# Order of four pieces of work around the mixer's end and the routing stage of an encoder layer

## The chip, the cores and the metric

The kernel runs on one core of a Trainium2 chip. The metric is the device time of one execution in microseconds (us), the median of three runs. The engines are named as in the profile: PE (matrix multiply, with PEld for its weight loads), DVE (vector), ACT (scalar, activation), POOL (GpSimd) and SP, which here only issues DMAs and reads a few registers for them.

## The reference, cut to what matters

```
mod = silu(c) @ w_ada + b_ada                   # six rows of 2048: sh1, sc1, g1, sh2, sc2, g2
h   = rms_norm(x, g_mix) * (1 + sc1) + sh1
z   = h @ w_in                                  # 2048 x 4616; the last 8 columns are the forget logits fz
y   = concat[gmlp(u, v), pool(p), forgetting_attention(q, k, va, fz)]      # the mixer
x   = x + g1 * (y @ w_out)
h   = rms_norm(x, g_ffn) * (1 + sc2) + sh2
scores = sigmoid(h @ w_router); top group of 4, then top 2 of its 4 experts, per token
x   = x + g2 * moe(h)                           # 16 experts: (silu(h @ e_gate) * (h @ e_up)) @ e_down
```

There are 256 tokens of 2048 values, 16 experts with an inner width of 1024, everything in float32. The output is x.

## The kernel before

**Stages.** In time order: (1) the first modulation rows, then the product with w_in, in five chunks of rows of w_in (256, 256, 512, 512, 512 rows, `CHUNKS`); (2) the mixer, woven into the last chunk (`LAST` is its order); (3) the product with w_out, four column blocks of 512, each from four loads of 512 rows (`wout_steps(n)`, steps `g`); (4) the router: norm, logits, choice, counts of tokens per expert, and a gather of the tokens into the order of the experts; (5) the experts, fifteen of them one after the other (`ORDER`), each with eight 2 MB loads of e_gate and e_up and four of e_down.

**Precision.** Products with w_in and w_out are made as three matmuls in a rounded format. ACT casts a weight tile to its high part, and DVE or POOL subtracts that from the tile for the low part (`split`, lines 175 and 176, tile `whl`, 128x2x512, six buffers). `WSO = "GVGG"` says which engine subtracts for the four rows of w_out's tile: POOL, DVE, POOL, POOL. One such step is six matmuls of 128x512 on PE (`mm3`, twice).

**Weights in flight.** Loads go through a ring of half buffers of 1 MB (`ring()`, `load_tile`, line 147), `ring0` to `ring2` with two halves each, and from stage 3 on also `ringm0`. A load into a half waits until what was in it has been read. In stage 5 the same buffers are used whole (2 MB), with two more (`ringl0`, `ringl1`) that take the place of the gather's inputs and so can be filled only when the gather is done. SP issues all weight loads, in program order.

**What sets the order.** Each engine runs its own list of instructions in program order, and the list follows the order of the Python code. A small queue, `todo`, holds matmul parts back: `step(prep, run)` runs `prep` at once (the load and the splits) and puts `run` (the matmuls) at the end of `todo`; while what is in it weighs over `LOOK = 4` (a split step 1, an unsplit one 2, anything else 0), the first entry is taken out and run. `then(f)` puts other work behind what waits there. `flush()` runs all.

**Forget logits.** `make_h(q)` (line 408) makes one chunk of h: per 128 columns, PE transposes, DVE scales (`hf`, line 420), ACT casts and DVE subtracts (`hT`). The 8 forget logits are small matmuls from `hf` into `lgp` (`late`), put into `todo` behind two entries.

**Gate 2.** The row g2 takes 16 loads of w_ada (sixteen unsplit steps, four per 512 columns; each is four matmuls with one output row, and every fourth step a bias matmul behind it and an ACT copy `r2[q]`). `G2 = [1, 2, 1, 1]` steps go beside the last block of w_out, `G2_MID = 1` behind it, `NG2` of them are put in ahead of the count matmuls, and `g2_run(16)` puts in the rest ahead of the gather. Because `todo` holds two unsplit steps back, the last two of those ahead of the counts run behind them. The broadcast of g2 to 128 rows (`g2w`: four matmuls with `sel` and four ACT copies) is first needed in the first expert's down stage.

**Counts.** The matmuls with `M` (the chosen experts) into `pp`, then `po`, give the order of the experts (`irow`, line 1089), which SP reads into a register before it can issue the first expert's load.

Of the kernel before, what the change touches and what calls it, by code (L numbers as in the profile page):

```python
# [63 lines left out]

LAST = ["mwm", "mwm", "mw", "mawmam", "amw", "mmmwammm", "ammam", "ammammgmx", "amvammm", "aamsmapmtmmmm"]

G2, G2_MID, NG2 = [1, 2, 1, 1], 1, 4

M1A, M1B, M2A, M2B, G1 = "PPVV", "PPPP", "PPPP", "PPPP", "PVVV"
WSPLIT, WSO = ["VGVG", "VGVG", "GVGG", "GVGG", "GVGG"], "GVGG"  # L70
# [12 lines left out]
def layout(tiles):  # L83
    out, o = {}, 0
    for key, r0, nr, c0, ncol in tiles:
        m = nr * ncol // 128
        out[key] = (o, m, r0, nr, c0, ncol)
        o += 128 * m
    return out
# [19 lines left out]
WOUT = layout(((n, g), 512 * g, 512, 512 * n, 512) for n in range(4) for g in range(4))  # L109
# [7 lines left out]
def body(tc, x_d, prm_d, bg_d, wada_d, win_d, wout_d, egu_d, ed_d, out_d):  # L117
# [32 lines left out]
    todo = deque()  # L150

    def run_first():
        f, x, _ = todo.popleft()
        f(x) if x is not None else f()
# [6 lines left out]
    def then(f):  # L161
        todo.append((f, None, False)) if todo else f()

    def flush():
        while todo:
            run_first()

    V, S, G, E = nc.vector, nc.scalar, nc.gpsimd, nc.tensor

    def mm(out, lhsT, rhs, start=True, stop=True):  # L170
        E.matmul(out, lhsT=lhsT, rhs=rhs, start=start, stop=stop, skip_group_check=True)  # L171
# [35 lines left out]
    sel = cst.tile([128, 128], F32, name="sel")  # L207
# [26 lines left out]
    pbanks = deque(psM.tile([128, 512], F32, name=f"pm{i}") for i in range(3))  # L234

    def pm():
        pbanks.rotate(-1)
        return pbanks[-1]
# [122 lines left out]
    def yhi(k):  # L361
        return hTs[0][:, (k - 8) // 4, k % 4, :] if k >= 8 else hTs[1][:, k // 4, k % 4, :]
# [22 lines left out]
    for g, w in enumerate((2, 4, 8, 16)):  # L385
        b = band0[:, g, :]
# [20 lines left out]
    def make_h(q):  # L407
        k0, nk = CHUNKS[q]
        hq = hbuf(q)
        ts = []  # L410
        for c in range(nk):
            k = k0 + c
            if c % 2 == 0:
                p2 = pt()
                for j in range(4):
                    o = 128 * (c + j // 2)
                    E.transpose(p2[:, 128 * j:128 * j + 128], xn[:, j % 2, o:o + 128], ident)
            p = p2[:, 256 * (c % 2):256 * (c % 2) + 256]
            t = wk.tile([128, T], F32, name="hf", bufs=5)
            V.tensor_scalar(t, p[:, :T], mod[:, 1, k:k + 1], mod[:, 0, k:k + 1], op0=OP.mult, op1=OP.add)  # L420
            split(hq[:, 0, c, :], hq[:, 1, c, :], t)
            ts.append((k, t))

        def late():
            for k, t in ts:
                o = 32 * (k % 4)
                mm(fzp[o:o + 8, :], wfz[:, k, :], t, start=k < 4, stop=k >= KD - 4)
        todo.insert(2, (late, None, False)) if todo else late()


    def halves(flat, tile, engs, xs, banks, first, last, after):
        buf = []

        def one(a):
            def prep():
                if a == 0:
                    w = ring()
                    load_tile(w, flat, tile)
                    buf.append(w.rearrange("p (k n) -> p k n", k=4))
                hl = hp.tile([128, 2, 512], F32R, name="whl")  # L440
                split(hl[:, 0], hl[:, 1], buf[0][:, a, :], engs[a])
                return hl

            def run(hl):
                P = banks()
                for h in range(2):
                    mm3(P[h], *xs(a, h), hl[:, 0], hl[:, 1], first and a == 0, last and a == 3)
                if a == 3:
                    after(P)
            step(prep, run, True)  # L450
        for a in range(4):
            one(a)
# [300 lines left out]
    ylo = py.tile([128, KD, T], F32R, name="ylo")  # L753
# [11 lines left out]
    def att(n):  # L765
        for _ in range(min(n, len(steps_a))):
            then(lambda i=steps_a.popleft(): att_step(i))

    for i, order in enumerate(LAST):
        if i < len(PIECES):  # L770
            piece(last, PIECES[i])
        for c in order:
            if c == "a":
                att(1)
            elif c == "m":
                mods(1)
            elif c == "w":
                for f in work.get(PIECES[i], ()):
                    then(f)
            else:  # L780
                then(named[c])
    att(11)
    mods(len(mod2))
    flush()
    while tbanks[-1] is not accs[0]:
        tbanks.rotate(-1)
    tbanks.pop()
# [60 lines left out]
    for w in (128, 64, 32, 0):  # L848
        n = CAPS.count(w)
# [2 lines left out]
    limR = rtile([128, 16], "limR")  # L852
    V.tensor_scalar(limR, capR, -1.0, 512.0, op0=OP.mult, op1=OP.add)

    WO = [{"V": V, "G": G}[c] for c in WSO]

    def wout_steps(n, Ps):
        def banks():
            if not Ps:
                Ps.extend(sets[n % 2])  # L860
            return Ps

        def one(g):
            def xs(c, h):
                k, s = 4 * g + c, slice(128 * h, 128 * h + 128)
                return yhi(k)[:, s], ylo[:, k, s]
            return lambda: halves(wout_d, WOUT[n, g], WO, xs, banks,
                                  g == 0, g == 3, lambda P: None)
        return [one(g) for g in range(4)]

    def x1_block(n, Ps, g1):
        for h in range(2):
            t = wk2.tile([128, 512], F32, name="xg")
# [63 lines left out]

    g1_load(1)
    pbanks.append(accs[1])
    sets = [list(pbanks)[:2], list(pbanks)[2:]]  # L940
    r2, g2p, g1s = [], deque(), {}

    def g2_run(n):
# [1 line left out]
            step(*g2p.popleft())  # L945

    for n in range(4):
        Ps = []
        ws = wout_steps(n, Ps)
        for g in range(4):  # L950
            ws[g]()
            if n + g:
                g1_load(1)
            if n == 3 and g == 0:
                r2 += [grow2() for _ in range(4)]
                for q in range(4):
                    g2p.extend(ada_parts(5, 4 * q, 4, lambda P, q=q: S.copy(r2[q], P), (accs[0], sets[0][0])[q % 2],
                                         4 + q))
            if n == 3:
                for _ in range(G2[g]):  # L960
                    step(*g2p.popleft())
            if n == 0 and g == 3:
                then(logit_const)
            if n == 3 and g == 2:
                then(lambda: S.activation(lnj, ones[:, 0:1], AF.Ln))
            if g == 1 and n > 0:
                then(lambda n=n: logit_a(n - 1))
            if g == 2:
                then(lambda n=n: g1s.__setitem__(n, g1_bc(n)))
                if n > 0:  # L970
                    then(lambda n=n: logit_b(n - 1))
        then(lambda n=n, Ps=Ps: x1_block(n, Ps, g1s[n]))
# [14 lines left out]
    g2w = pg2.tile([128, D], F32, name="g2w")  # L987
# [130 lines left out]

    g2_run(16)
    flush()  # L1120

    for b in range(4):
        p = pm()
        mm(p, sel, r2[b])
        S.copy(g2w[:, 512 * b:512 * b + 512], p)
    def gather(k):

        p = pm()
# [54 lines left out]
    for h in range(2):  # L1183
# [4 lines left out]
        pick(gatO[:, h, :], ohO, gatR[:, h, :])  # L1188
        V.tensor_tensor(posR[:, h, :], posR[:, h, :], dlt, op=OP.add)

    s_phl.close()
    pl, s_pl = pool("pl", 1, side="right")
    wides += [pl.tile([128, 2 * RINGW], F32, name=f"ringl{i}") for i in range(RING_LAST)]
# [269 lines left out]
```

## Time and profile before

| | |
|---|---|
| median of three runs | 1419.65 us (1417.56 to 1420.41) |
| profiled execution | 1422.95 us, span 1421.1 us |
| PE busy | 1209.0 us, 85% of the span |
| DVE, ACT, POOL busy | 590.9, 363.6, 216.1 us |
| DMA | 539.14 MB, mean 379 GB/s |
| TensorE clock, mean granted | 0.957 |

The profile is one execution. Times are us from the span's start. In a timeline a row gives start, length, engine, source line, operation, what is written from what, how many instructions are merged, and in brackets how long the engine had been idle before and what released it. A granted clock of 1.00 is 2.4 GHz and 0.50 is 1.2 GHz. Line 171 is the helper of all matmuls, lines 175 and 176 those of all splits, so tile names tell what a row is.

### The profile page before, as it was taken

The numbers are of one execution on the slowest core, as the hardware profiler recorded it, in microseconds if no ns is written. First come the engines' busy times: TensorE is split into PE (matmuls) and PEld (weight loads), VectorE is DVE, ScalarE is ACT, GpSimd is POOL, SyncE is SP. The second block draws the span as 40 slices with busy tenths as digits, with TensorE's granted clock in tenths as the row PEclk, the third lists the DMA queues.
The fourth block names the chain that finished last, engine by engine and source line by source line (L and its number), as shares of the span: only waits on it lengthen the run. The fifth ranks groups of instructions, "written<-read, shape, count | busy, mean of one in ns | idle before, by whom it ended". The sixth has DMA issues, their size and how long they took to land.

```text
span 1421.1 us, 17044 instructions
## 1 busy us (share of the span) xinstructions
PE 1209.0 (85%) x6646; PEld 628.8 (44%) x6646; DVE 590.9 (42%) x1121; ACT 363.6 (26%) x661; POOL 216.1 (15%) x170
## 2 busy tenths in 40 slices
PE   5999999999899787999969999688885888858866
PEld 2656766665676352763326743222232222322221
DVE  4366544655784734882327942121130211302112
ACT  4633433445444241770006820000000000000000
POOL 1345654522675000000000000000000000000000
PEclk9999999999999898999989999899998999989997
DMA  9988695889979689998999989999999999999996
GB/s 390 362 342 336 255 369 217 309 341 354 366 306 368 218 370 428 427 380 355 427 426 427 423 310 429 425 427 427 427 426 427 427 427 428 426 427 427 426 427 266
DMA packets 49222, 539.14 MB, mean 379 GB/s; under 512 B 5472, under 2 KB 5600, under 8 KB 7024
## 3 DMA queue, kind: packets, MB, share of 16 engines
q1 hardware_dynamic: 47664, 534.79, 92.0%
q10 hardware_dynamic: 1472, 3.19, 0.6%
q8 instruction: 55, 0.90, 0.3%
q14 instruction: 31, 0.25, 0.1%
HBM read 535.86 MB, written 2.10 MB: 379 GB/s over the span
## 4 chain that ended last, share of the span: by engine, by line
PE 56%; DMA 33%; DVE 4%; issue 3%; ACT 2%; POOL 1%; SPq 0%; DVEq 0%; POOLq 0%; ACTq 0%
PE lbank L171 25%; PE pm L171 18%; DMA ring<-in_e_down_dram 13%; DMA ringm<-in_e_gu_dram 10%; DMA ring<-in_e_gu_dram 9%; PE ada L171 6%; PE bank L171 4%; PE pt L171 1%; DMA ring<-in_w_ada_dram 1%; POOL whl L176 1%; DVE el L176 0%; DVE hf L420 0%; PE pt L327 0%; DMA bgt<-in_bg_dram 0%; ACT hT L175 0%
## 5 line engine op out<-in xcount | busy, mean ns | idle before, releaser
L171 PE MATMUL pm<-whl,hT 128*128 128x512 f32 x1056 | 278.6, 401 | 10.0 <-DVE whl L176 6.9
L171 PEld LDWEIGHTS pm<-whl,hT 128*128 128x128 f32 x1056 | 198.1, 191 | 74.2 <-issue 11.0
L171 PE MATMUL lbank<-ring,xr 128*32 128x256 f32 (+1 forms) x1216 | 158.3, 505 | 44.0 <-DMA ring<-in_e_gu_dram 44.0
L176 POOL TENSOR_TENSOR whl<-ring,whl 128x512 fp32r<-128x512 f32 x116 | 159.3, 1393 | 178.1 <-ACT whl L175 173.8
L171 PE MATMUL bank<-y,gt 128*128 128x512 f32 x240 | 119.6, 621 | 0.0
L171 PEld LDWEIGHTS lbank<-ring,xr 128*32 128x32 f32 (+1 forms) x1216 | 56.3, 130 | 137.8 <-issue 66.2
L1344 DVE TENSOR_TENSOR xa<-xa,bank 128x512 f32<-128x512 f32 x120 | 82.5, 688 | 74.4 <-PE bank L171 74.4
L171 PE MATMUL lbank<-ringl,xr 128*32 128x256 f32 (+1 forms) x608 | 81.4, 520 | 35.5 <-DMA ringl<-in_e_gu_dram 35.5
L175 ACT CAST whl<-ring 128x512 fp32r<-128x512 f32 x164 | 94.6, 621 | 60.8 <-PE pm L171 47.3
L171 PE MATMUL lbank<-ring,hidT 128*64 128x512 f32 (+1 forms) x416 | 84.9, 716 | 28.4 <-DVE hidT L1303 16.7
L1335 DVE TENSOR_TENSOR y<-lbank,g2w 128x512 f32<-128x512 f32 x60 | 41.5, 692 | 154.4 <-PE lbank L171 154.4
L171 PE MATMUL lbank<-el,xs 128*128 128x512 f32 x384 | 94.3, 405 | 7.1 <-ACT el L175 5.2
L171 PE MATMUL lbank<-ringm,xr 128*32 128x256 f32 (+1 forms) x608 | 75.7, 472 | 21.7 <-DMA ringm<-in_e_gu_dram 20.8
L1231 ACT COPY gt<-bank 128x256 f32<-128x256 f32 x15 | 5.6, 372 | 337.7 <-PE bank L1229 337.7
L1285 DVE TENSOR_TENSOR hid<-hid,lbank 128x512 f32<-128x512 f32 x11 | 7.6, 688 | 201.8 <-PE lbank L171 201.7
L171 PEld LDWEIGHTS lbank<-el,xs 128*128 128x128 f32 x384 | 73.6, 194 | 27.8 <-ACT el L175 7.4
L460 DVE TENSOR_TENSOR z<-z,pm 128x512 f32<-128x512 f32 x72 | 49.1, 688 | 68.9 <-PE pm L171 68.9
L171 PE MATMUL ada<-ring,cact 128*1 128x512 f32 (+1 forms) x520 | 62.5, 580 | 17.4 <-DMA ring<-in_w_ada_dram 14.2
L171 PE MATMUL lbank<-ringl,hidT 128*64 128x512 f32 (+1 forms) x416 | 74.2, 598 | 1.3 <-DMA ringl<-in_e_down_dram 1.3
L171 PEld LDWEIGHTS bank<-y,gt 128*128 128x128 f32 x240 | 41.9, 192 | 74.1 <-issue 71.7
L1280 DVE TENSOR_TENSOR hid<-hid,lbank 128x256 f32<-128x256 f32 x6 | 2.5, 422 | 165.5 <-PE lbank L171 140.0
L171 PEld LDWEIGHTS lbank<-ringl,xr 128*32 128x32 f32 (+1 forms) x608 | 28.8, 133 | 86.9 <-DMA ringl<-in_e_gu_dram 50.7
(389 smaller groups left out, 1264.1 us busy)
## 6 DMA issues: line engine op xcount, KB each, us to landing
ring<-in_e_gu_dram SPq DMA_DIRECT2D x60, 2048.0 KB, 24.6
ring<-in_w_ada_dram SPq DMA_DIRECT2D x81, 1024.0 KB, 7.3
ringm<-in_e_gu_dram SPq DMA_DIRECT2D x30, 2048.0 KB, 25.5
ringl<-in_e_gu_dram SPq DMA_DIRECT2D x30, 2048.0 KB, 25.0
ring<-in_e_down_dram SPq DMA_DIRECT2D x30, 2048.0 KB, 24.7
ringl<-in_e_down_dram SPq DMA_DIRECT2D x30, 2048.0 KB, 25.8
ring<-in_w_in_dram SPq DMA_DIRECT2D x28, 1024.0 KB, 7.1
ring<-in_w_out_dram SPq DMA_DIRECT2D x12, 1024.0 KB, 8.2
```

What stands on the lines that cost most here:

```text
L171: E.matmul(out, lhsT=lhsT, rhs=rhs, start=start, stop=stop, skip_group_check=True)
L175: S.copy(hi, src)
L176: (eng or V).tensor_tensor(lo, src, hi.bitcast(F32), op=OP.subtract)
L460: V.tensor_tensor(dst, dst, P[h], op=OP.add)
L1231: S.copy(gt, p[:, :256])
L1280: V.tensor_tensor(hid[:, :256], hid[:, :256], P[1][:, :256], op=OP.mult)
L1285: V.tensor_tensor(hid[:, o], hid[:, o], P[2 * b + 1], op=OP.mult)
L1335: V.tensor_tensor(y, P, g2w[:, c0:c0 + 512], op=OP.mult)
L1344: V.tensor_tensor(a, a, p, op=OP.add)
```

## The change

Four edits. (1) `late` goes into `todo` behind six entries instead of two. (2) `wout_steps` and its list are made earlier, and the first of block 0's four steps is called ahead of the mixer's end: its load and its four splits are put in there, and its matmuls stay in `todo` until the mixer's matmuls are through (the loop takes the place of `flush()`). Its two PSUM banks are drawn there (`pair0`) and kept as one of the two sets. (3) `NG2` is 8 instead of 4. (4) The broadcast of g2 stands behind the gather and the rest of the routing arithmetic instead of ahead of them.

```diff
-G2, G2_MID, NG2 = [1, 2, 1, 1], 1, 4
+G2, G2_MID, NG2 = [1, 2, 1, 1], 1, 8
...
-        todo.insert(2, (late, None, False)) if todo else late()
+        todo.insert(6, (late, None, False)) if todo else late()
...
+    def wout_steps(n, Ps):
+        def banks():
+            if not Ps:
+                Ps.extend(pair0 if n == 0 else sets[n % 2])
+            return Ps
...
     att(11)
     mods(len(mod2))
-    flush()
+
+    Ps0, pair0 = [], [pm(), pm()]
+    ws0 = wout_steps(0, Ps0)
+    ws0[0]()
+    while len(todo) > 4 or todo[0][1] is None:
+        run_first()
...
-    sets = [list(pbanks)[:2], list(pbanks)[2:]]
+    sets = [pair0, [t for t in pbanks if not any(t is x for x in pair0)]]
...
     for n in range(4):
-        Ps = []
-        ws = wout_steps(n, Ps)
+        Ps = [] if n else Ps0
+        ws = wout_steps(n, Ps) if n else ws0
         for g in range(4):
-            ws[g]()
+            if n + g:
+                ws[g]()
...
     g2_run(16)
     flush()
-
-    for b in range(4):
-        p = pm()
-        mm(p, sel, r2[b])
-        S.copy(g2w[:, 512 * b:512 * b + 512], p)
     def gather(k):
...
+    for b in range(4):
+        p = pm()
+        mm(p, sel, r2[b])
+        S.copy(g2w[:, 512 * b:512 * b + 512], p)
     s_phl.close()
```

What this does to the engines' lists is shown at three places. First PE, where the third chunk of h is made: the last two split steps of the old chunk, the forget logits (`lgp`), and the first steps of the new one (`hT1`). Before:

```order
L171 MATMUL pm1_120<-whl_723,hT0_132 128x512 x3
L171 MATMUL pm2_121<-whl_723,hT0_132 128x512 x3
L171 MATMUL lgp_117<-hf_762,prm1_69 8x256
L171 MATMUL lgp_117<-hf_766,prm1_69 8x256
L171 MATMUL lgp_117<-hf_774,prm1_69 8x256
L171 MATMUL lgp_117<-hf_778,prm1_69 8x256
L171 MATMUL pm0_119<-whl_735,hT1_133 128x512 x3
L171 MATMUL pm1_120<-whl_735,hT1_133 128x512 x3
L171 MATMUL pm0_119<-whl_744,hT1_133 128x512 x3
L171 MATMUL pm1_120<-whl_744,hT1_133 128x512 x3
```

and now:

```order
L171 MATMUL pm1_120<-whl_723,hT0_132 128x512 x3
L171 MATMUL pm2_121<-whl_723,hT0_132 128x512 x3
L171 MATMUL pm0_119<-whl_735,hT1_133 128x512 x3
L171 MATMUL pm1_120<-whl_735,hT1_133 128x512 x3
L171 MATMUL pm0_119<-whl_744,hT1_133 128x512 x3
L171 MATMUL pm1_120<-whl_744,hT1_133 128x512 x3
L171 MATMUL pm0_119<-whl_747,hT1_133 128x512 x3
L171 MATMUL pm1_120<-whl_747,hT1_133 128x512 x3
L171 MATMUL lgp_117<-hf_762,prm1_69 8x256
L171 MATMUL lgp_117<-hf_766,prm1_69 8x256
L171 MATMUL lgp_117<-hf_774,prm1_69 8x256
L171 MATMUL lgp_117<-hf_778,prm1_69 8x256
```

The logits moved behind three steps of the new chunk here (three at the second chunk, two at the fourth and the fifth, where `todo` holds less).

Second POOL, at the mixer's end: the mixer's last two operations (`z`), then index rows (IOTA) for the router and w_out's splits (`whl`). Before:

```order
L579 TENSOR_TENSOR z_145<-z_145,hrv_2538 128x512
L655 TENSOR_TENSOR z_145<-z_145,prm2_71 128x512
L827 IOTA io512_2691 128x512
L829 IOTA iow_2693 128x128
L831 IOTA ioR_2695 128x256
L833 IOTA ioE_2697 128x256
L835 IOTA rev_2699 128x16
L837 IOTA ec_2701 16x1
L176 TENSOR_TENSOR whl_2724<-ring0_63,whl_2724 128x512
L176 TENSOR_TENSOR whl_2730<-ring0_63,whl_2730 128x512
L176 TENSOR_TENSOR whl_2737<-ring0_63,whl_2737 128x512
```

and now:

```order
L579 TENSOR_TENSOR z_145<-z_145,hrv_2538 128x512
L655 TENSOR_TENSOR z_145<-z_145,prm2_71 128x512
L176 TENSOR_TENSOR whl_2640<-ring2_65,whl_2640 128x512
L176 TENSOR_TENSOR whl_2666<-ring2_65,whl_2666 128x512
L176 TENSOR_TENSOR whl_2681<-ring2_65,whl_2681 128x512
L848 IOTA io512_2704 128x512
L850 IOTA iow_2706 128x128
L852 IOTA ioR_2708 128x256
L854 IOTA ioE_2710 128x256
L856 IOTA rev_2712 128x16
L858 IOTA ec_2714 16x1
```

Three of the first step's splits now stand ahead of the index rows. On ACT its first cast stands ahead of the mixer's last four casts (`hT`), the other three behind them and ahead of the load of the bias rows `bgt`; on DVE its one split stands ahead of the last modulation row's reduction (line 329).

Third PE in the routing stage: gate 2's steps (one output row, `cact`), the count matmuls (`M`), and what follows. Before:

```order
L171 MATMUL pm1_120<-bgt2_2689,ident_77 1x512
L171 MATMUL pt1_123<-M_3614,one2_2703 128x16 x2
L171 MATMUL pt1_123<-one2_2703,M_3614 16x1 x2
L171 MATMUL pt1_123<-M_3614,stri2_2705 128x16 x2
L171 MATMUL pt1_123<-M_3614,one2_2703 128x16
L171 MATMUL pt0_122<-ohc_3646,ec_2701 128x16
L171 MATMUL ada0_113<-ring1_64,cact_126 1x512 x4
L171 MATMUL ada0_113<-ring2_65,cact_126 1x512 x4
L171 MATMUL ada0_113<-ringm0_2677,cact_126 1x512 x8
L171 MATMUL ada0_113<-bgt2_2689,ident_77 1x512
L171 MATMUL pm1_120<-ring2_65,cact_126 1x512 x4
L171 MATMUL pm1_120<-ring0_63,cact_126 1x512 x8
```

and now:

```order
L171 MATMUL pm0_119<-bgt2_2702,ident_77 1x512
L171 MATMUL ada0_113<-ring1_64,cact_126 1x512 x4
L171 MATMUL ada0_113<-ring2_65,cact_126 1x512 x8
L171 MATMUL ada0_113<-ringm0_2690,cact_126 1x512 x4
L171 MATMUL ada0_113<-bgt2_2702,ident_77 1x512
L171 MATMUL pt1_123<-M_3614,one2_2716 128x16 x2
L171 MATMUL pt1_123<-one2_2716,M_3614 16x1 x2
L171 MATMUL pt1_123<-M_3614,stri2_2718 128x16 x2
L171 MATMUL pt1_123<-M_3614,one2_2716 128x16
L171 MATMUL pt0_122<-ohc_3668,ec_2714 128x16
L171 MATMUL pm0_119<-ringm0_2690,cact_126 1x512 x4
L171 MATMUL pm0_119<-ring0_63,cact_126 1x512 x8
```

Four of the eight steps that stood behind the counts stand ahead of them now. In both lists the last steps from `ring1` and their bias matmul follow; then before came the four matmuls with `sel` and the 64 of the gather (`oneh`), and now the gather and the four with `sel`. The first expert's loads go into the buffers in the order ringm0, ring2, ring0, ring1 before and ring2, ringm0, ring0, ring1 now, then ringl0 and ringl1 in both.

## Rows read from the trace of the kernel before

**Rows 1.** The page: span, data rate in 40 equal slices, one line of DMA issues

```profile
span 1421.1 us, 17044 instructions
...
GB/s 390 362 342 336 255 369 217 309 341 354 366 306 368 218 370 428 427 380 355 427 426 427 423 310 429 425 427 427 427 426 427 427 427 428 426 427 427 426 427 266
...
ring<-in_w_out_dram SPq DMA_DIRECT2D x12, 1024.0 KB, 8.2
```

**Rows 2.** Timeline of PE, forget logits of chunks three, four and five

```profile
98.43 0.60 PE L171 MATMUL lgp<-hf,prm 128*8 128x256 f32 x2 [0.70 <-DVE hf L420]
99.78 0.60 PE L171 MATMUL lgp<-hf,prm 128*8 128x256 f32 x2 [0.75 <-DVE hf L420]
...
159.56 0.60 PE L171 MATMUL lgp<-hf,prm 128*8 128x256 f32 x2 [0.75 <-DVE hf L420]
...
224.73 0.60 PE L171 MATMUL lgp<-hf,prm 128*8 128x256 f32 x2 [0.76 <-DVE hf L420]
```

**Rows 3.** Timeline of PE at the start of w_out

```profile
357.43 0.50 PE L171 MATMUL pm<-whl,hT 128*128 128x512 f32 x1 [1.22 <-ACT whl L175]
...
362.67 1.22 PE L171 MATMUL pm<-whl,hT 128*128 128x512 f32 x2 [1.69 <-DVE whl L176]
...
368.04 0.61 PE L171 MATMUL pm<-whl,hT 128*128 128x512 f32 x2
```

**Rows 4.** Timelines of DVE, ACT, POOL and SP around the mixer's end

```profile
361.07 0.94 DVE L802 TENSOR_TENSOR grow<-grow,bgt 1x512 f32<-1x512 f32 x1 [0.81 <-DMA bgt<-in_bg_dram]
...
355.83 0.30 ACTq L821 DMA_DIRECT2D bgt<-in_bg_dram  x1
...
357.53 7.45 POOL L176 TENSOR_TENSOR whl<-ring,whl 128x512 fp32r<-128x512 f32 x5
...
316.35 23.07 SPq L147 DMA_DIRECT2D ring<-in_w_ada_dram  x10
```

**Rows 5.** Two-microsecond windows: busy us of the engines, granted clock, DMA share, GB/s

```profile
360.00:362.00 2.00, 0.98 (x3) 0.26 (x1) 1.20 (x3) 0.62 (x1) 2.00 (x3) 0.50 0.99 378
...
366.00:368.00 2.00, 2.00 (x9) 1.61 (x8) 1.30 (x1) 0.62 (x1) 0.92 (x2) 0.84 0.95 365
...
478.00:480.00 2.00, 0.30 (x2) 0.30 (x2) 1.76 (x9) 0.48 (x2) 0.00 (x0) 0.82 1.00 422
...
488.00:490.00 2.00, 2.00 (x16) 0.30 (x8) 1.88 (x5) 0.00 (x0) 0.00 (x0) 0.62 0.00 0
```

**Rows 6.** Chain of waits: start, length, engine and tile; w_out, four steps

```profile
380.17 5.48 PE pm L171 x24
```

**Rows 7.** Waits of PE from 362 to 466: total, times, longest

```profile
PE pm L171 <- DVE whl L176: 1.7, 1, 1.7
```

**Rows 8.** Groups of DVE, 362 to 441: busy, mean ns, idle before and releaser

```profile
L297 DVE SCALAR_TENSOR_TENSOR ada<-ring,cact,ada 128x512 f32<-128x512 f32 x33 | 24.9, 754 | 1.0
L176 DVE TENSOR_TENSOR whl<-ring,whl 128x512 fp32r<-128x512 f32 x10 | 12.5, 1248 | 13.1 <-ACT whl L175 13.1
```

**Rows 9.** Timeline of PE in the routing stage: counts, gate 2, broadcast, gather's last matmuls

```profile
479.70 1.03 PE L171 MATMUL pt<-M,one 128*128 128x16 f32 x4 [3.76 <-DVE M L1050]
...
483.89 3.59 PE L171 MATMUL ada<-ring,cact 128*1 128x512 f32 x16
...
496.38 2.84 PE L171 MATMUL pm<-grow,sel 128*128 128x512 f32 x6 [0.67 <-ACT grow L957]
...
513.57 1.07 PE L171 MATMUL ada<-oneh,xhl 128*128 128x512 f32 x4
```

**Rows 10.** Timelines of DVE and SP in the routing stage

```profile
484.00 0.16 DVE L1089 CAST irow<-pt 1x16 int32<-1x16 f32 x1 [0.70 <-PE pt L171]
...
493.17 0.75 DVE L1116 SCALAR_TENSOR_TENSOR oneh<-io,sl,oneh 128x512 fp32r<-128x512 f32 x1
...
490.34 0.35 SPq L1352 DMA_DIRECT2D ringm<-in_e_gu_dram  x1
...
514.76 0.87 SPq L1352 DMA_DIRECT2D ringl<-in_e_gu_dram  x2
```

More of the change, by code (lines that the diff above doesn't have):

```diff
@@ L781, in body, with one, xs @@
                 then(named[c])
+    WO = [{"V": V, "G": G}[c] for c in WSO]
+    def wout_steps(n, Ps):
[3 more added lines that the diff above has]
+            return Ps
+        def one(g):
+            def xs(c, h):
+                k, s = 4 * g + c, slice(128 * h, 128 * h + 128)
+                return yhi(k)[:, s], ylo[:, k, s]
+            return lambda: halves(wout_d, WOUT[n, g], WO, xs, banks,
+                                  g == 0, g == 3, lambda P: None)
+        return [one(g) for g in range(4)]
     att(11)
     mods(len(mod2))
-    flush()
+    Ps0, pair0 = [], [pm(), pm()]
[3 more added lines that the diff above has]
+        run_first()
     while tbanks[-1] is not accs[0]:
@@ L853, in body @@
     V.tensor_scalar(limR, capR, -1.0, 512.0, op0=OP.mult, op1=OP.add)
[L855 to L869, printed above, removed]
     def x1_block(n, Ps, g1):
```

## The prediction

> **What bounds the kernel now.** I read the data rate first. In [rows 1] it lies between 217 and 390 GB/s in the first 15 of the 40 slices (35.5 us each) and from then on at 423 to 430, but for dips in two expert stages and the last slice. So from about 516 us (the first load into `ringl` goes out at 514.76, [rows 10]) the kernel waits for its expert weights, 24 MB per expert, and the order of that part does not change. Every microsecond by which the loads run gapless earlier comes off the end, and nothing else in that part can. Ahead of it the rate is lower and PE works nearly all the time, so that part is a chain through PE and, in the routing stage, DVE. Next I read the timelines for where PE waits ahead of 516 us. There are three such places, and the change touches each. At the forget logits PE waits for `hf` of a column that DVE has yet to make, 0.70 to 0.76 us at a time [rows 2]. At the start of w_out it waits for ACT, then for DVE [rows 3], and its clock falls [rows 5]. In routing it waits 3.76 us for the choice of experts `M` [rows 9], then runs gate 2's remaining steps at half clock, and the first expert load goes out only at 490.34 though the order of the experts has been there since 484.16 [rows 10].
>
> **The change part by part.** The profiled execution took 1422.95 us for a span of 1421.1, 3.3 over the median of 1419.65. I make the sum against the former and take 3.3 off.
>
> *Forget logits.* No instruction is added; a full chunk's four logit matmuls move behind two or three steps of six matmuls, each of which needs only one column (128 wide) of the new chunk. Columns come every 1.35 us (99.78 less 98.43, [rows 2]); a step takes 5.48 / 4 = 1.37 us [rows 6]. So steps follow the columns as these are made, and the logits, all inputs long ready, no longer wait, and take the time that they took before. The waits that go are 0.70 + 0.75 + 0.75 + 0.76 = 2.96 us. The second chunk, with two columns, I count at nothing. Above 3 us it can hardly give more; below nothing it cannot go, since nothing reads the logits before the last chunk and `hf` has five buffers for at most four columns. It gives nothing where POOL's splits, which start only behind the new chunk's casts, hold PE up instead; I take 3.0, range 0.5 to 3.5.
>
> *w_out's first step.* The same load, four casts and four subtractions are made earlier; the cost is what they stand in front of. Now PE is free at 357.43 - 1.22 = 356.21 and has no split [rows 3]. POOL makes its index rows first and starts splitting at 357.53 [rows 4]. DVE's second-row split stands behind `grow`, which waits for `bgt`; that load is issued at 355.83 and its reader starts at 361.07 [rows 4]. So PE has a third of the step done when it stops until 362.67; the clock stays at 0.50 until within 366 to 368 [rows 5]. The step's 24th matmul ends at 368.04 + 0.23 = 368.3. In the changed kernel all four splits are made while PE does the mixer's last matmuls, and 24 matmuls from 356.21 take 5.48 [rows 6]: 361.7, without the fall of the clock. That is 6.6 us. Off this comes what is late next, the second step's split on DVE: `grow` still ends at 361.07 + 0.94 = 362.0, its own split takes 1.25 more beside POOL [rows 8], and the index rows that DVE reads ahead of `grow` come after three POOL splits now, so 363.3 to 364.7. PE wants it two matmuls into the second row, 361.7 + 8 x 0.228 = 363.5. I take off 1.1 and keep 5.5.
>
> What hides the moved work: w_out's first load goes out as the last of the ten issues that end at 339.42 instead of behind them [rows 4]; with 8.2 us to land [rows 1] it is there at 348, eight us ahead of PE's first need of it at 356.21. If that cover were gone, ACT would stand at its first cast with the mixer's last four behind it, and PE would be late by as much as the load is. Afterwards PE waits once in 100 us, at the place just removed [rows 7], and DVE waits 13.1 us for casts that wait for PE to free a split buffer [rows 8]; the stage is PE's, so its end moves with its start. Bounds: 0, if the stage gives it all back, and 6.6.
>
> *Eight steps of gate 2, broadcast behind the gather.* Four steps and a bias matmul move from behind the counts to in front of them. Two of these steps take 3.59 us at half clock [rows 9], so four take 3.6 at full clock, and I allow 0.9 for the bias. PE has 3.76 us there. The counts start up to 0.9 late, but PE no longer idles ahead of them: the clock fell within 478 to 480 and came back within 488 to 490 [rows 5], and the counts, now at full clock, win back 1.5 of the 4.3 us to `irow` (479.70 to 484.00, [rows 9, 10]). Net 0.5 us earlier; bounds 0.9 later and 1.5 earlier. SP's first expert load then waits for `irow` only, at about 485 instead of 490.34; but four loads of 2 MB (2.1 million bytes) at 427 GB/s take 19.7 us, so they are through by about 507, and the next two wait for the end of the gather (514.76, where the gather's matmuls end at 513.57 + 1.07 = 514.64, [rows 9, 10]). So the end of the gather decides, and what the earlier load gains is hidden.
>
> The gather waits for `oneh`, ready at 493.92 [rows 10], but starts at about 500 because gate 2's last copies and the broadcast, from 496.38 on [rows 9], stand ahead. In the changed kernel the remaining four steps are through by 489 (`irow` at 483.7, and 4.5 us) and the gather starts at 493.4. Its 64 matmuls take 64 x 0.228 = 14.6 us, to 508.0, if the clock is full. But PE now idles from 489 to 493.4. In the rows such idling brought half clock: the fall within 478 to 480 came in the 3.76 us without a matmul, and after 362.67 it took 4 us of work to come back [rows 3, 5, 9]. Four microseconds at half clock cost 2.0, so 510.0, against 514.64: 4.6 us. Bounds: no fall 6.6; half clock for 9.3 us, as in 479 to 488.5, 2.0. The Trainium skill has the same as a rule (TensorE: Matmul & The Clock Gate, HAM oscillation): a matmul engine that is left idle too long restarts at half rate and must be kept busy to get back. By it alone the fall is to be expected here, as the trace shows it; a result of its own is the second rival below. The broadcast itself, 3.5 us by four copies and matmuls, now stands ahead of the first expert's matmuls, which start near 514;  the two loads that go out at 510 keep the queue full until 520, and the next follow PE's reads of the first buffers well ahead of that, so this costs nothing.
>
> Sum: 3.0 + 5.5 + 4.6 = 13.1. 1422.95 - 13.1 = 1409.85; less 3.3, **1406.5**.
>
> **The rivals.** *The w_out stage gives its head start back.* DVE's sums for gate 1 or the loads would then set its pace. For it: its DVE list is dense. Against it: [rows 7, 8]. Time: 1406.5 + 5.5 = 1412.0.
>
> *The gather runs at half clock throughout.* Then 29.2 us instead of 14.6 plus 2.0: 12.6 more, 1419.1, no change. For it: PE idles ahead of it, and around the counts the clock stayed low for some 9 us though PE worked through most of them [rows 5]. Against it: the gather is dense, and dense work brought the clock back in 4 us.
>
> *Slower: DVE becomes the bound of w_out.* The mechanism is POOL and DVE side by side: splits moved ahead and PE at full pace make them overlap more. If each of the 48 sums of gate 1 (33 of them in [rows 8], 754 ns) took the 1248 ns of a split, DVE would need 23.7 us more, 13.1 of which is its idle time: the stage ends 10.6 later than before. 1422.95 - 3.0 + 10.6 - 4.6 - 3.3 = 1422.7. It decides from 0.754 + 13.1 / 48 = 1.03 us per sum. Against it: the sums kept 754 ns over the very stretch in which the splits took 1248. The Trainium skill (GPSIMD Engine Reference, 1. Specifications) says POOL shares its memory interfaces with the vector engine, in contention with vector instructions that have two inputs in that memory. [...]
>
> *The change doesn't do what it says.* The logits go two or three steps back, not six, because `todo` holds no more; priced above as it is. Where POOL holds PE up all the same, their 3.0 are gone: 1409.5, inside the first case's range.
>
> **How the numbers follow.** Forecast 0.75, given back 0.12, half clock 0.05, slower 0.04; 0.04 is left for what I haven't seen, half of it faster. The forecast's own range takes its parts near their bounds, not all at once: 1402 to 1411. With the first rival whole and part of the second, and on the other side the best of all parts (3.5 + 6.6 + 6.6 = 16.7), the range for 8 in 10 is 1402 to 1414. A measurement of this kernel tells 0.2% (2.8 us) from no change, so faster means under 1416.8: 0.75 + 0.12 + 0.02 and a share of half clock that is only partial, 0.91 in all; same 0.05; slower 0.04.
>
> **What would show it.** Logits: no wait of PE for `hf` beyond the first chunk. w_out: matmuls without a gap from the mixer's last one, and the granted clock 1.00 through 360 to 368 (about 3 us earlier in time); the stage's end 8 to 9 us earlier, at 456 to 457 instead of 465. Routing: gate 2's second-last bank ahead of the counts, the first expert load some 14 us earlier, the gather directly behind `oneh`, the two loads behind it at about 501, and from then on the same 425 to 428 GB/s. I am wrong if the w_out stage shows new waits of PE for DVE or for loads, if the counts wait for a load of gate 2, or if the gather's matmuls stay at 0.4 us and more.

## The result and the profile after

The changed kernel takes 1408.73 us (median of 12 runs), the kernel before 1419.38 in the same series; the ratio is 0.9936 with a 95% interval of 0.9923 to 0.9949, so 7 to 11 us are gone. 13.1 had been forecast. The time lies inside the range, but one of the three terms is not there: the late logits gain nothing.

The page of the changed kernel, span and data rate, answers to [rows 1]:

```profile
span 1412.5 us, 17042 instructions
...
GB/s 390 348 347 291 291 360 209 322 359 341 374 336 369 285 366 428 427 379 370 427 427 426 416 315 428 426 428 427 426 427 426 428 426 427 426 426 429 425 425 263
```

The part behind the first `ringl` load is as long as it was, to a microsecond: 1412.5 - 506.8 = 905.7 us, against 1421.1 - 514.8 = 906.4. In all fourteen traces of this case it is 902.8 to 906.4. So the account has to be settled ahead of that load, in three stages. The execution profiled took 1414.28 us.

**Stage 1, the logits.** The timelines of PE and of DVE in the changed kernel, chunk three; they answer to [rows 2].

```profile
95.28 3.67 PE L171 MATMUL pm<-whl,hT 128*128 128x512 f32 x15
102.35 6.29 PE L171 MATMUL pm<-whl,hT 128*128 128x512 f32 x15 [3.40 <-DVE z L460]
108.58 0.62 PE L171 MATMUL lgp<-hf,prm 128*8 128x256 f32 x8
```

```profile
100.27 0.54 DVE L420 TENSOR_SCALAR hf<-pt,mod 128x256 f32<-128x256 f32 x1
101.28 0.43 DVE L176 TENSOR_TENSOR hT<-hf,hT 128x256 fp32r<-128x256 f32 x1 [0.47 <-ACT hT L175]
101.62 1.28 DVE L460 TENSOR_TENSOR z<-z,pm 128x512 f32<-128x512 f32 x2
```

The waits for `hf` are gone from this chunk, and in their place stands one of 3.40 us. PE runs the last two steps of the old chunk and half of the first new one (15 matmuls). The other half writes a bank `pm` that the old chunk's steps have filled too (there are three banks), and DVE's sums `z` have to empty it first. DVE has those sums behind all four columns of the new chunk. And then the clock falls, in two-microsecond windows of the same trace (columns as in [rows 5]):

```profile
100.00:102.00 2.00, 0.00 (x0) 0.00 (x0) 1.53 (x4) 1.16 (x3) 0.16 (x1) 0.78 0.11 45
102.00:104.00 2.00, 1.65 (x4) 1.36 (x5) 1.67 (x3) 0.81 (x2) 2.00 (x2) 0.50 0.03 8
106.00:108.00 2.00, 2.00 (x6) 1.58 (x5) 0.00 (x0) 0.62 (x1) 0.71 (x2) 0.52 0.62 262
```

The 15 matmuls behind the wait take 6.29 us; the 15 ahead of it took 3.67. At the end of stage 1, taken here as the start of the 55th of DVE's 72 sums `z`, behind the last chunk's columns, this execution is 2.9 us behind the kernel before: 237.33 against 234.43. Of this 0.3 was there at the first of these sums, ahead of all that the late logits change. The distance is 3.1 still at the mixer's last sums (355.83 against 352.76).

**Stage 2, w_out's start.** The timeline of PE in the changed kernel; it answers to [rows 3].

```profile
359.21 0.50 PE L171 MATMUL pm<-whl,hT 128*128 128x512 f32 x1
...
367.67 0.73 PE L171 MATMUL pm<-whl,hT 128*128 128x512 f32 x2 [0.89 <-DVE whl L176]
```

The first step follows the mixer without a gap; one wait of 0.89 us comes in the second step, at the place where the prediction had put it, for a split that DVE has behind `grow`. From the mixer's last sums (`ylo`) to w_out's last (`xg`) it is 107.93 us, against 113.27: 5.3 less. In a second trace of the same kernel (run 10) the wait is not there, and the stage takes 106.79: 6.5 less.

**Stage 3, routing.** Timelines of PE, DVE and SP in the changed kernel; they answer to [rows 9, 10].

```profile
476.16 1.04 PE L171 MATMUL ada<-ringm,cact 128*1 128x512 f32 x8
477.13 1.02 PE L171 MATMUL ada<-bgt,ident 8*1 8x512 f32 x2
478.07 0.62 PE L171 MATMUL pt<-M,one 128*128 128x16 f32 x4
...
482.86 4.72 PE L171 MATMUL pm<-ring,cact 128*1 128x512 f32 x24
...
490.19 4.74 PE L171 MATMUL pm<-oneh,xhl 128*128 128x512 f32 x12 [1.67 <-DVE oneh L1122]
...
505.65 1.07 PE L171 MATMUL ada<-oneh,xhl 128*128 128x512 f32 x4
506.56 2.74 PE L171 MATMUL pm<-grow,sel 128*128 128x512 f32 x6
```

```profile
481.31 0.16 DVE L1095 CAST irow<-pt 1x16 int32<-1x16 f32 x1 [0.69 <-PE pt L171]
...
489.30 0.75 DVE L1122 SCALAR_TENSOR_TENSOR oneh<-io,sl,oneh 128x512 fp32r<-128x512 f32 x1
```

```profile
482.29 0.35 SPq L1358 DMA_DIRECT2D ring<-in_e_gu_dram  x1
...
506.84 0.87 SPq L1358 DMA_DIRECT2D ringl<-in_e_gu_dram  x2
```

Gate 2's second-last bank is done ahead of the counts, and the gather directly behind the first half of `oneh`. From `M` (477.17) to the gather's end (505.65 + 1.07 = 506.72) it is 29.55 us; before it was 514.64 - 479.46 = 35.18: 5.6 less.

### The profile page after: what moved, and what is told of

The parts are those of the page before. It is cut to its first block, busy times and chain, and to the rows that moved or that the text cites. A ratio compares the mean times of both kernels' runs of the same rounds, so it can differ in the third digit from the quotient of the medians.

```text
span 1412.5 us, 17042 instructions
## 1 busy us (share of the span) xinstructions
PE 1207.9 (86%) x6646; PEld 627.1 (44%) x6646; DVE 592.7 (42%) x1121; ACT 363.4 (26%) x661; POOL 216.9 (15%) x170
## 4 chain that ended last, share of the span: by engine, by line
PE 51%; DMA 35%; issue 4%; DVE 4%; ACT 2%; POOL 2%; SPq 0%; DVEq 0%; POOLq 0%; ACTq 0%
PE lbank L171 23%; PE pm L171 16%; DMA ring<-in_e_down_dram 15%; DMA ring<-in_e_gu_dram 14%; PE ada L171 5%; PE bank L171 4%; DMA ringl<-in_e_down_dram 2%; POOL whl L176 2%; DMA ringl<-in_e_gu_dram 2%; PE pt L171 1%; DMA ringm<-in_e_gu_dram 1%; DMA ring<-in_w_ada_dram 1%; DVE el L176 0%; ACT whl L175 0%; DMA bgt<-in_bg_dram 0%
## 5 line engine op out<-in xcount | busy, mean ns | idle before, releaser
L176 POOL TENSOR_TENSOR whl<-ring,whl 128x512 fp32r<-128x512 f32 x116 | 160.8, 1408 | 181.8 <-ACT whl L175 177.5
L171 PE MATMUL lbank<-ringm,xr 128*32 128x256 f32 (+1 forms) x608 | 81.8, 520 | 21.2 <-DMA ringm<-in_e_gu_dram 21.2
L171 PE MATMUL lbank<-el,xs 128*128 128x512 f32 x384 | 91.1, 395 | 6.2 <-ACT el L175 4.1
L171 PE MATMUL ada<-ring,cact 128*1 128x512 f32 (+1 forms) x536 | 63.8, 575 | 16.3 <-DMA ring<-in_w_ada_dram 13.1
L175 ACT CAST el<-ring 128x512 fp32r<-128x512 f32 x96 | 57.4, 622 | 50.0 <-DMA ring<-in_e_gu_dram 42.9
```

The source lines that it names most:

```text
L175: S.copy(hi, src)
L176: (eng or V).tensor_tensor(lo, src, hi.bitcast(F32), op=OP.subtract)
```

## The experiments

Each kernel is the changed kernel with the edit shown, unless said. They ran in three series (1 to 4; 5 to 8; 9 to 12), each with the kernel before beside it, and the ratios are to that.

**1. The logits back.**

```diff
-        todo.insert(6, (late, None, False)) if todo else late()
+        todo.insert(2, (late, None, False)) if todo else late()
```

> The changed kernel with the forget logits put back behind two entries of the queue. Theory A (from the two traces): the late logits cost time. In the changed kernel PE reaches the third piece step of chunk three and then waits 3.40 us for a DVE sum z, because DVE has that sum behind all four columns of the new chunk, and the clock is at 0.50 for the 15 matmuls behind the wait; at the end of stage 1 the changed kernel is 2.9 us behind the kernel before. So putting the logits back should make it faster by 2.9 us: 1405.8 against 1408.7, with the waits of 0.70 to 0.76 us back and none of 3.4. Theory B (the prediction): the late logits gain 3.0, and this kernel is at 1411.7. If the loss is made good later by other waits: 1408.7, no change.

Measured: 1411.2 us, ratio 0.9944 (0.9923 to 0.9966), which is 1407.5 to 1413.6 us. The 1405.8 of theory A is excluded. Theory B's 1411.7 is nearest, but the interval holds no change as well, so this run does not tell these two apart; experiment 9 does. The trace says why a size is hard to get: the waits of 0.69 and 0.75 are back and no wait of 3.4, but this time the clock fell in the wait of 2.60 us at 119 to 122, where it had not fallen in the kernel before or the changed one, and stage 1 ends at 237.25. One profiled execution is one draw of where the clock falls.

**2. Logits of two chunks left out, in the kernel before.**

```diff
-        todo.insert(2, (late, None, False)) if todo else late()
+        if q not in (2, 3):
+            todo.insert(2, (late, None, False)) if todo else late()
```

> The kernel before, with the forget logits of chunks three and four left out altogether (16 small matmuls; the forget gate then comes from the other chunks alone). Theory A: the logit waits were not lost time in chunk three, since PE has to wait there for DVE's sum z in any case; without the logits it waits once and for longer (about 3.4 us), its clock falls, and 15 matmuls at half clock cost some 2.8 us. Chunk four, where the sums stand ahead of the columns, gains about 1.4 + 0.6. So the kernel is 0.5 to 2 us slower than before although work is left out. Theory B: the waits and the logits are lost time; the kernel is faster by 0.70 + 0.75 + 0.75 and the 16 logits (16 x 0.14 = 2.2), 4.4 us in all: 1415.0 against 1419.4.

Measured: 1419.58 us, ratio 1.0010 (0.9994 to 1.0026), which is from 0.9 us faster to 3.7 slower. Theory A's 0.5 to 2 slower lies inside, and 4.4 faster is excluded: leaving the logits out gains at most 0.9. Timeline of PE in chunk three:

```profile
94.39 3.69 PE L171 MATMUL pm<-whl,hT 128*128 128x512 f32 x15
101.47 6.86 PE L171 MATMUL pm<-whl,hT 128*128 128x512 f32 x23 [3.39 <-DVE z L461]
```

With no logits at all PE waits for the same sums. So the logits of chunk three filled a wait for DVE, in the kernel before, that is there without them.

**3. The broadcast ahead of the gather again.**

```diff
     g2_run(16)
     flush()
+    for b in range(4):
+        p = pm()
+        mm(p, sel, r2[b])
+        S.copy(g2w[:, 512 * b:512 * b + 512], p)
...
-    for b in range(4):
-        p = pm()
-        mm(p, sel, r2[b])
-        S.copy(g2w[:, 512 * b:512 * b + 512], p)
```

> The changed kernel with the broadcast of g2 put back ahead of the gather; gate 2's eight steps stay. Theory A (from the trace after): PE idles from 488.5 to 490.19 ahead of the gather and runs its first 12 matmuls at half clock (4.74 us for 2.88). The broadcast in that place takes the idle time from 489.2 to 492.6 and keeps the clock, so the gather, at full clock, ends within 0.5 us of 506.7: no change against 1408.7. Theory B (the prediction's sum): the gather waits for the broadcast's 3.5 us, less the idle time of 1.7, so it ends 1.8 to 2.5 us later: 1410.5 to 1411.2.

Measured: 1409.89 us, ratio 0.9943 (0.9923 to 0.9963). PE's timeline:

```profile
483.60 2.84 PE L171 MATMUL pm<-grow,sel 128*128 128x512 f32 x6 [0.68 <-ACT grow L963]
...
486.73 3.33 PE L171 MATMUL pm<-oneh,xhl 128*128 128x512 f32 x12
```

The broadcast stands in what was idle time, and the gather's first 12 matmuls take 3.33 us instead of 4.74. `M` to the gather's end: 30.12 us, 0.6 more than changed. By the stage this is theory A, nearly to the number; the interval of the whole time holds both theories.

**4. Four steps ahead of the counts, broadcast behind the gather.**

```diff
-G2, G2_MID, NG2 = [1, 2, 1, 1], 1, 8
+G2, G2_MID, NG2 = [1, 2, 1, 1], 1, 4
```

> The changed kernel with four steps of gate 2 ahead of the counts as before instead of eight; the broadcast stays behind the gather. Four steps more stand between the counts and the gather, there at half clock, and PE idles ahead of the counts. Theory A: gate 2's last bank ends at about 493.4 (495.7 in the kernel before, less the 2.3 us by which this stage starts earlier), the gather starts there without idle time and at full clock, and ends at 508.0 against 506.7: 1.3 us slower, 1410.0. Theory B (the edit's gain is the whole of the 5.7 us found in this stage): 1414.4. If only the broadcast mattered: 1408.7.

Measured: 1410.88 us, ratio 0.9940 (0.9918 to 0.9961); `M` to the gather's end 30.26 us, 0.7 more than changed. So by the stage each of the two routing edits alone gives about 5.0 of the 5.6 us, and the second adds 0.6: theory A, with half its price. The whole time excludes theory B's 1414.4, but not that nothing was lost.

**5. w_out's first step back.**

```diff
-    Ps0, pair0 = [], [pm(), pm()]
-    ws0 = wout_steps(0, Ps0)
-    ws0[0]()
-    while len(todo) > 4 or todo[0][1] is None:
-        run_first()
+    flush()
```

The banks and the loop over the blocks are as in the kernel before, too.

> The changed kernel with w_out's first step put back behind the mixer's end (and the queue emptied there, as before); the other three edits stay. Theory A (from the two traces, as predicted): the stage from the mixer's last sums (ylo) to w_out's last sums (xg) is 5.3 us longer in the kernel before than in the changed one (113.27 against 107.93), so it is back at 113.3 and the kernel at 1408.7 + 5.3 = 1414.0. Theory B: the stage gets its pace from elsewhere (loads or DVE's sums) and the head start is lost in it or in the loads behind: under 2 us slower, 1410.7 at most.

Measured: 1415.14 us, ratio 0.9985 (0.9971 to 1.0000), 6.4 more than the changed kernel of run 10, by the medians of two series. The stage takes 113.22 us, and PE's timeline has the waits of [rows 3] again:

```profile
355.85 0.50 PE L171 MATMUL pm<-whl,hT 128*128 128x512 f32 x1 [1.22 <-ACT whl L175]
...
357.27 0.73 PE L171 MATMUL pm<-whl,hT 128*128 128x512 f32 x2 [0.69 <-POOL whl L176]
...
361.09 1.22 PE L171 MATMUL pm<-whl,hT 128*128 128x512 f32 x2 [1.53 <-DVE whl L176]
```

**6 and 7. Columns interleaved on DVE**, with the logits behind two entries (6) and late (7).

```diff
-            split(hq[:, 0, c, :], hq[:, 1, c, :], t)
+            S.copy(hq[:, 0, c, :], t)
             ts.append((k, t))
+            if c > 0:
+                V.tensor_tensor(hq[:, 1, c - 1, :], ts[c - 1][1], hq[:, 0, c - 1, :].bitcast(F32), op=OP.subtract)
+        V.tensor_tensor(hq[:, 1, nk - 1, :], ts[nk - 1][1], hq[:, 0, nk - 1, :].bitcast(F32), op=OP.subtract)
```

> The changed kernel with the logits behind two entries again, and DVE's two operations on a column of the new chunk interleaved: it scales the next column while ACT casts this one, and subtracts behind that. Theory A: DVE's list is what PE waits for in stage 1, in the logits' waits as in the sums' (z). A column takes DVE 1.35 us now, of which 0.47 is a wait for ACT's cast; without that 0.9, so four columns are made 1.3 us sooner and the sum behind them comes 1.3 us sooner. PE's waits of 0.70 to 0.76 us for hf go or shrink to a third; stage 1 is 2 to 3.5 us shorter than with the logits put back, apart from what the clock does, so the kernel is at 1405.5 to 1409. Theory B: something else holds PE there too (POOL's splits start only behind the casts of the columns), stage 1 is shorter by under 1 us and the time is that of the kernel with the logits put back, 1411.

> The same interleaved columns with the logits as late as in the changed kernel. Theory A: the wait for z of 3.40 us in chunk three falls by 1.3 to about 2.1 and the one of 1.17 in chunk two by 0.45; the columns still stand ahead of the sum on DVE, so the late logits gain nothing against the kernel with interleaved columns and logits behind two entries (within 1 us). Theory B (the prediction): the late logits gain 3 us against it.

Measured: 6 takes 1402.70 us, ratio 0.9891 (0.9874 to 0.9909); 7 takes 1406.61, ratio 0.9922 (0.9907 to 0.9937). PE's and DVE's timelines in 6, chunk three:

```profile
91.72 2.47 PE L171 MATMUL pm<-whl,hT 128*128 128x512 f32 x10
94.11 1.32 PE L171 MATMUL lgp<-hf,prm 128*8 128x256 f32 x8
```

```profile
93.46 0.54 DVE L420 TENSOR_SCALAR hf<-pt,mod 128x256 f32<-128x256 f32 x1
93.92 0.41 DVE L424 TENSOR_TENSOR hT<-hf,hT 128x256 fp32r<-128x256 f32 x1
94.25 0.54 DVE L420 TENSOR_SCALAR hf<-pt,mod 128x256 f32<-128x256 f32 x1
```

A column now takes 94.25 - 93.46 = 0.79 us instead of 1.35, and all eight logit matmuls run with no wait that the row marks. Stage 1 ends at 225.68. The gain is larger than theory A had it: DVE's sums `z` come 1.9 us sooner in each of the three full chunks, 5.7 in all; the rest of the distance to run 1 in stage 1 lies in chunk one and in where the clock falls. And the late logits cost 3.9 us by the medians (the intervals of the ratios just touch) where B had them gain 3: in 7 a wait for `z` is still in chunk three, in 6 there is none. In the two traces stage 1 ends 2.8 us apart: 1.5 are lost in chunks two and three, nothing is won behind them, and the rest is one more fall of the clock in 7. PE's timeline in 7:

```profile
97.09 3.69 PE L171 MATMUL pm<-whl,hT 128*128 128x512 f32 x15 [1.47 <-DVE z L463]
```

**8. The columns' subtractions on POOL**, logits behind two entries.

```diff
-            split(hq[:, 0, c, :], hq[:, 1, c, :], t)
+            split(hq[:, 0, c, :], hq[:, 1, c, :], t, G)
```

> The changed kernel with the logits behind two entries and the subtractions of the columns (hT) made by POOL, which has nothing to do for 6 to 8 us at that place. Theory A: DVE has four operations of 0.54 for a chunk and then its sums z, some 3 us sooner than now, and the logits never wait; the low parts of the columns come every 0.7 us or so from POOL, faster than the 1.35 of now. PE's waits for hf and z in chunks two and three go; stage 1 is 3 us shorter than with the logits put back, apart from the clock, and the kernel at 1405 to 1408. Theory B: POOL's splits of w_in are then late by the 2 to 3 us that the columns take there, PE waits for POOL instead, and the kernel is at 1411 or slower.

Measured: 1402.67 us, ratio 0.9897 (0.9879 to 0.9914), stage 1 ends at 224.06. DVE's timeline:

```profile
92.88 1.90 DVE L420 TENSOR_SCALAR hf<-pt,mod 128x256 f32<-128x256 f32 x4
94.69 1.27 DVE L460 TENSOR_TENSOR z<-z,pm 128x512 f32<-128x512 f32 x2
```

The sums come 1.81 us after the first column instead of 5.4 (101.62 - 96.21 in the changed kernel). Theory A, and below its 1405 to 1408; against experiment 6 there is no difference in the whole time. In both, routing gives a part back: from `M` to the gather's end it is 33.8 us in 6 and 32.4 in 8, against 29.55 in the changed kernel. Gate 2's eight steps ran partly at half clock and held the counts 4.2 and 2.5 us behind `M`, and the gather's first 12 matmuls took 5.72 us. PE's timeline in 6, then in 8:

```profile
480.53 5.72 PE L171 MATMUL pm<-oneh,xhl 128*128 128x512 f32 x12 [2.74 <-DVE oneh L1125]
```

```profile
477.26 5.72 PE L171 MATMUL pm<-oneh,xhl 128*128 128x512 f32 x12 [4.43 <-DVE oneh L1122]
```

**9. Late logits alone, in the kernel before** (the edit of experiment 1 the other way round).

> The kernel before with the first edit alone: logits behind six entries. Theory A (after the runs so far): without the clock the late logits are worth nothing, since chunks two and three lose 0.85 each to waits for sums that stand behind the columns and chunks four and five win 1.0 and 0.55 back; with the clock, which fell in the 3.4 us wait of chunk three in three traces of four and costs 1.7 to 3.4 us when it does, they cost 1 to 3 us: 0 to 3 us slower than before. Theory B (the prediction): 3.0 us faster than before.

Measured: 1420.87 us, ratio 1.0012 (0.9996 to 1.0028): from 0.6 us faster to 4.0 slower. A gain of 3.0 is excluded; a loss is not shown. Stage 1 ends at 237.34, 2.9 late as in the changed kernel.

**10. The changed kernel again.**

> The changed kernel once more, unaltered, beside the others of this call: 9 to 11 us faster than before, as measured before (ratio 0.9936), and the level from which the two last ones are counted.

Measured: 1408.75 us, ratio 0.9932 (0.9913 to 0.9950). PE's timeline in chunk three:

```profile
95.00 3.69 PE L171 MATMUL pm<-whl,hT 128*128 128x512 f32 x15
102.08 3.71 PE L171 MATMUL pm<-whl,hT 128*128 128x512 f32 x15 [3.38 <-DVE z L460]
...
123.22 5.53 PE L171 MATMUL pm<-whl,hT 128*128 128x512 f32 x16 [2.60 <-DVE whl L176]
```

The same kernel and the same wait, and the clock did not fall there: 3.71 us for what took 6.29. It fell in the next wait, of 2.60 us: 5.53 us for 16 matmuls that took 3.93 in the first trace of this kernel. Of the seven traces with this wait (changed, again, and runs 2, 3, 4, 5, 9) it fell in four.

**11 and 12. What the runs point to:** experiment 8 with the broadcast ahead of the gather (11), and with `NG2 = 6` besides (12).

> What the runs point to: logits behind two entries, the columns' subtractions on POOL, w_out's first step early, eight steps of gate 2 ahead of the counts, and the broadcast of g2 ahead of the gather again. In the run with the columns on POOL PE idles for 4.43 us ahead of the gather (472.8 to 477.26) and the gather's first 12 matmuls take 5.72 us for 2.88. Theory A: the broadcast's 3.5 us fit into that idle time and keep the clock, so the gather ends 2 to 3 us sooner than there: 1400 against 1402.7. Theory B: the gain of the edit that put the broadcast behind the gather is lost: 3.5 us slower, 1406.

> The same with six steps of gate 2 ahead of the counts instead of eight. In the run with the columns on POOL the counts start at 465.35 though the choice M is there at 463.02, because gate 2's eight steps are not through; six would let the counts start with M, 2.3 us sooner, and the two other steps fill PE's idle time ahead of the gather. Theory A: the choice of tokens and the gather come 1 to 2 us sooner than with eight: 1399. Theory B: the two steps and the broadcast together (4 + 3.5 us) now stand in front of the gather longer than DVE takes to make its input: same time as with eight, or 1 us slower.

Measured: 11 takes 1402.19 us, ratio 0.9882 (0.9861 to 0.9904); 12 takes 1406.06, ratio 0.9912 (0.9894 to 0.9930). PE's timeline in 11, then in 12:

```profile
472.03 2.84 PE L171 MATMUL pm<-grow,sel 128*128 128x512 f32 x6 [0.68 <-ACT grow L963]
...
476.89 2.55 PE L171 MATMUL pm<-oneh,xhl 128*128 128x512 f32 x10 [0.39 <-DVE oneh L1122]
```

```profile
467.60 1.95 PE L171 MATMUL ada<-ringm,cact 128*1 128x512 f32 x8
...
481.03 3.33 PE L171 MATMUL pm<-oneh,xhl 128*128 128x512 f32 x12
```

In 11 the gather ends 14.40 us behind `oneh` instead of 16.90 in run 8 (491.23 - 476.83, 495.20 - 478.30), which is theory A for the stage; the whole time, 1402.2 against 1402.7 in another series, doesn't tell the two kernels apart; it does exclude theory B's 1406. 12 is theory B and worse: two steps more behind the counts, at half clock (a step in 1.95 us for what takes 1.04), push the gather back, which ends 496.15 - 476.63 = 19.5 us behind `oneh`. Version 11 has the lowest median, not told apart from 8 and 6: 1.2% under the kernel before, 0.5% under the changed one.

## Why the prediction came out as it did

The time came out 2.2 us above the forecast. That it is no more is in part luck: the 3.0 us of the logits were not there, and the two other terms, each about 1 us larger than forecast, made up for part of them.

**The end and the bound: right.** What the `ringl` loads go out earlier came off the end, to within the spread of 3.6 us of what follows them in all traces (902.8 to 906.4).

**w_out: right.** 5.5 forecast, with bounds of 0 and 6.6; 5.3 and 6.5 in two traces, 6.4 by undoing it. The clock stayed at 1.00 from 360 to 368, as it was to show. The split that was to be late next was late in the one (0.89 us; 1.1 had been taken off), not in the other. The rivals on this stage (head start given back, DVE as the bound) are out: the stage is 106.8 us in all nine other traces of kernels that keep this edit. That the stage's end came only 2.3 us earlier in the first trace (463.76 against 466.03), and not 8 to 9, is stage 1's loss.

**Routing: right, slightly small.** 4.6 forecast, 5.6 found. The half clock at the gather's start costs 4.74 - 2.88 = 1.9 us (2.0 forecast), 2.88 being what 12 of its matmuls take later on, so the rival of half clock throughout is out. The missing 1.0 is that the gather's first matmuls need only the first half of `oneh`, done 1.2 us ahead of the second. `irow` comes 0.4 us sooner behind `M` (4.14 against 4.54; 0.5 forecast). What I did not see is that the two edits pay for the same thing: either alone brings 5.0. Nor did I see that gate 2's steps ahead of the counts can hold these up by far more than 0.9 us when the clock is low there (4.2 and 2.5 in experiments 6 and 8).

**Logits: wrong.** The step that failed is "steps follow the columns as these are made, and the logits, all inputs long ready, no longer wait", with its bound "below nothing it cannot go". It looked only at the splits and the columns, as inputs of the steps, and not at their output: the first new step writes a bank that has to be emptied, and in chunk three DVE does so behind the four columns (in chunk two ACT does, and PE waits 1.17 us for it). The waits of [rows 2] in chunk three were PE's share of a wait for DVE that is there with the logits or without (experiment 2), and the logits filled part of it. Chunks four and five, where the sums stand ahead of the columns, did gain, 1.4 and 0.9 us at first, as DVE's sums `z` show (4.47 us late falls to 3.06, 3.44 to 2.51). PE then waits 0.24 and 0.63 us for POOL's splits, the limit that the prediction had named, and 0.4 of each gain goes again: 1.0 and 0.55 are left. Chunk two lost 0.75, chunk three 3.4 in the first trace and 0.8 in run 10, where the clock held in this wait.

So where the clock holds in chunk three the four chunks together come to nothing: stage 1 ends at 234.51 in run 10 and at 234.43 in the kernel before. The two are fair to compare, as both start the second chunk's sums at the same time and each has one fall of the clock behind that, in a wait of 2.60 us: run 10 at 123, the kernel before here:

```profile
185.20 5.51 PE L171 MATMUL pm<-whl,hT 128*128 128x512 f32 x16 [2.60 <-DVE whl L176]
```

Where it falls in chunk three, 2.6 us are lost. By the whole time the late logits make the kernel before something between 0.6 us faster and 4.0 slower (experiment 9), where 3.0 faster was forecast. Experiment 1, by its ratio against the changed kernel's, points 1 us the other way, with an interval that holds both signs. So the gain of 3.0 is refuted, and the sign of what remains is open.

With -6.4 for w_out, -5.6 for routing and 0 to +1.7 (the middle of experiment 9) for the logits the sum is -12.0 to -10.3, against 10.65 between the medians, with 7 to 11 by the interval.

Not settled: how often the clock falls in that wait over many executions, since seven traces are few; and whether experiments 6, 8 and 11 differ.

## What to carry to other kernels

When an engine waits for another one's list, moving the waiting instruction back does not remove the wait: ask what the next instruction waits for in the same list, its output buffer included. Shorten the list instead; interleaving two instructions on DVE gave some 8 us here (experiment 6 against 1), where moving the logits on PE gave nothing. Small work that stands in such a wait is free there. It can keep the clock up, too, as the broadcast of g2 did ahead of the gather (experiments 3 and 11).

## What the hardware showed

The fall of TensorE's clock is not fixed by the program: the same kernel, waiting 3.40 and 3.38 us at the same place, went to 0.50 in one execution and stayed at 1.00 in another, 2.6 us apart. Waits of 2.60 to 2.73 us, of which every trace has two between 115 and 189, brought the fall in 14 of 28. This moves the end of stage 1 by several microseconds (232.76 to 237.33 in five traces of kernels that are alike up to there: changed, 10, 3, 4 and 5); about 2 of these are lost in chunk one already, where the first 24 matmuls with w_in took 6.0 us in some traces and 7.4 in others.

The length of the wait alone does not decide it. Ahead of the gather the fall came every time: in the seven traces with eight steps ahead of the counts and the broadcast behind, PE idled 1.5 to 4.4 us there and the granted clock over the gather's first 12 matmuls was 0.50 to 0.66. In the three with the broadcast in this place it was 1.00.

The Trainium skill (TensorE: Matmul & The Clock Gate, HAM oscillation) has it that an engine left idle too long restarts at half rate; the traces agree where the clock fell, and show that with stage 1's waits of 2.6 to 3.4 us it is so in a part of the executions only.
